# A sixth weight tile for the experts, placed in memory that the router has given back, and scaled outputs moved to a shared scratch tile

## The chip, the cores and the metric

The kernel runs on one core of a Trainium2 chip. The metric is device microseconds of one execution, the median of several; lower is better. In the text PE is the matmul engine (PEld its weight load), DVE the vector engine, ACT the scalar engine, POOL GpSimd, and SP the sync engine, whose queue issues nearly all weight loads.

## The reference

Two blocks run one after the other on 256 tokens of width 1024, all in float32. The first block (depth 1) is a mixer of three branches, a cross attention and a feed-forward layer. The second block has two layers, each a token mixer and then a mixture of experts, which is the part that matters here:

```
def hierarchical_moe(h, w_grp, b_grp, w_exp, b_exp, w_gate, w_up, w_down):
    ...
    for gi in range(N_GROUPS):
        sl = slice(gi * EXPERTS_PER_GROUP, (gi + 1) * EXPERTS_PER_GROUP)
        hid = jax.nn.silu(jnp.einsum('td,edf->tef', t, w_gate[sl])) * jnp.einsum('td,edf->tef', t, w_up[sl])
        y = y + jnp.einsum('tef,efd->td', hid * combine[:, sl, None], w_down[sl])
```

Each layer has 32 experts. An expert has three matrices of 1024 x 256 floats (1 MiB each). The router picks two experts for every token, and `combine` holds their weights. The result is scaled per column by a gate vector and added to x.

## The kernel before

All 96 expert matrices of a layer are read once, whatever the router picks. `ExpertLoads` reads them in loads of three matrices, one from each of three experts in a row: gate 0, up 0, then for j = 1 to 10 gate j, down j-1, up j, and last down 10. These are 33 loads for a layer; a load is three DMAs of 1 MiB (two for j = 10), all issued by SP. A load goes into a tile of three places, 24 KiB in each partition. Five such tiles (`ring0` to `ring4`) are used in turn, so a load has to wait until the matmuls have finished with the tile that it overwrites. In this text "load n" counts these loads from 1 in each layer.

SP runs its queue in order. Three loads are issued while the mixer before is still at work, two more (`for _ in range(2): loads.load()`) when the last memory of the mixer comes free. The router then works: logits, the best group, the two best experts, ranks of tokens within an expert, and the weights `comb`. Its tiles are in a pool `pro`, opened as `pr`. The last of these tiles to be read is `csel`, in the reduction at L1751, inside the first step of `group(0)`.

The work on the experts goes in 11 groups j of three experts and a fourth set of slots for overflow, 32 token slots each. `group(j)` gathers the tokens of the slots into `XT` with one-hot matrices `Sg`; `gate(j)` and `up(j)` multiply them with the weights (L1631), `mid(j)` transposes, `down(j)` multiplies with the third matrix (L1815), and `scatter(j)` adds the outputs to four banks `yb` over all groups. The order on PE is written out by hand: gate(j), group(j+1), down(j-1), up(j), scatter(j-1), mid(j). After each down product DVE scales half the output by the gate vector (`od`, L1821), ACT rounds it to a high part (`oh`, L1822), and DVE makes the low part (`ol`, L1823). The pool `pmoe`, opened after the router, holds these tiles twice.

`junk` is one scratch tile of 128 x 1024 for the whole kernel, and `jf` a pair of 128 x 256 scratch tiles. At the end of a layer a branch tests whether an expert got more tokens than its slots hold; if so, `overflow` works through all experts again. In the profiled execution it is not entered.

Of the kernel before, what the change touches and what calls it, by code (L numbers as in the profile page):

```python
# [9 lines left out]
F32 = mybir.dt.float32  # L10
# [5 lines left out]
P = 128  # L16
S = 256
D = 1024
# [120 lines left out]
class Net:  # L139
# [1520 lines left out]
    def moe(self, l):  # L1660
        tc, nc, V, C = self.tc, self.nc, self.V, self.C
        v, act, te = nc.vector, nc.scalar, nc.tensor
        A, x, ident, mod = self.A, self.x, self.ident, self.mod[l]
        with ExitStack() as c:
# [4 lines left out]
            ring = [(c, self.ctx)[l].enter_context(tc.tile_pool(name="ring%d" % i, bufs=1, side="right", reuse_waits="tile"))  # L1669
                    for i in range(5)]  # L1670
# [3 lines left out]
            loads = self.ExpertLoads(self, l, 3)  # L1674
# [13 lines left out]
            idx = pe.tile([P, 12], I32, name="idx")  # L1688
            for _ in range(2):
                loads.load()  # L1690
            pr = c.enter_context(tc.tile_pool(name="pro", bufs=1, reuse_waits="tile"))


            wg = pr.tile([P, KT, 40], F32, name="wg")
# [35 lines left out]
            route = self.route(l, pr, lg, comb, rank, sel, idx)  # L1730
            next(route)
            yb = [[self.bank("yb") for _ in range(2)] for _ in range(2)]
            pm = c.enter_context(tc.tile_pool(name="pmoe", bufs=2, reuse_waits="tile"))
            hold = {}

            def group(j):
# [39 lines left out]
            def weights(j):  # L1776

                w = loads.get()
                return [w[:, bass.ds(ats[j], 1)].rearrange("p o n -> p (o n)")] + [w[:, i] for i in (0, 1, min(2, 31 - 3 * j))]
# [28 lines left out]
            def down(j, hd):  # L1808
                wds = weights(j)
                bks = [self.bank(), self.bank()]  # L1810
                for h in range(2):
                    for f in range(2):
                        for i in range(4):
                            ps = slice(i * 32, i * 32 + 32)
                            te.matmul(bks[h][ps, :], hd[:, f, ps], wds[i][:, f * D + h * 512:f * D + h * 512 + 512],  # L1815
                                      start=f == 0, stop=f == 1)
                os = []
                for h in range(2):
                    t = pm.tile([P, 512], F32, name="od")
                    o = Split(pm.tile([P, 512], F32R, name="oh"), pm.tile([P, 512], F32R, name="ol"))  # L1820
                    v.tensor_tensor(t, bks[h], self.gb[:, h * 512:h * 512 + 512], op=OP.mult)  # L1821
                    act.activation(o.hi, t, AF.Copy)  # L1822
                    v.tensor_tensor(o.lo, t, o.hi, op=OP.subtract)  # L1823
                    os.append(o)
                return os
# [9 lines left out]
                skip_runtime_bounds_check_because="idx is 2 a + b of two flags of which at most one is set")  # L1835
            for _ in group(0):
                pass
            self.gb = self.gate_rows(pe, l, 1)
            with tc.manual_schedule(engines={mybir.EngineType.PE}):
                for j in range(12):  # L1840
                    if j < 11:
                        th = gate(j)
                    for _ in group(j + 1) if j < 10 else ():
                        pass
                    if j:
                        os = down(j - 1, hd)
                    if j < 11:
                        up(j, th)
                    if j:
                        scatter(j - 1, ST, os)  # L1850
                    if j < 11:
                        hd, ST = mid(j, th)
# [24 lines left out]
    def overflow(self, l, pm, xn, ga, bb, comb, rank, sel):  # L1877

        tc, nc, C, A = self.tc, self.nc, self.C, self.A
        v, act, te = nc.vector, nc.scalar, nc.tensor  # L1880
        x = self.x
        co = pm.tile([P, 2, 33], F32, name="co", bufs=1)
        cur = pm.tile([P, 1], F32, name="cur", bufs=1)
        c4 = co.rearrange("p t (j i) -> p t j i", i=3)
        v.scalar_tensor_tensor(c4, sel.unsqueeze(1).to_broadcast([P, 2, 11, 3]), -32.0, rank[:, :, :, 1:],
                               op0=OP.mult, op1=OP.add)
        v.scalar_tensor_tensor(co, co, 32.0, comb, op0=OP.is_ge, op1=OP.mult)
        v.tensor_scalar(co, co, 0.5, None, op0=OP.mult)
        v.memset(cur, 0.0)
        with tc.For_i(0, 32, 1) as e:  # L1890
            hT, wg, wu, wd, th = [self.wtile() for _ in range(5)]
            self.rest = []
            hT = hT.rearrange("p (k t) -> p k t", k=KT)
            for tt in range(2):
                for k in range(KT):
                    bk = self.bank()
                    te.transpose(bk[:, :P], xn[:, tt, k], self.ident)
                    v.tensor_scalar(hT[:, k, tt * P:(tt + 1) * P], bk[:, :P], ga[:, k:k + 1], bb[:, k:k + 1],
                                    op0=OP.mult, op1=OP.add)
            for w, nm, k, n in ((wg, "w_gate_2", 8, 256), (wu, "w_up_2", 8, 256), (wd, "w_down_2", 2, D)):  # L1900
                nc.sync.dma_start(w[:, :2048].rearrange("p (k n) -> p k n", k=k),
                                  A[nm][l, bass.ds(e, 1)].rearrange("o (p k) n -> p (o k) n", p=P))
            cv = pm.tile([P, 2], F32, name="cv", bufs=1)
            t = pm.tile([P, 2, 32], F32, name="ct2", bufs=1)
            for tt in range(2):
                v.scalar_tensor_tensor(t[:, tt], C["iota"][:, :32], cur, co[:, tt, :32], op0=OP.is_equal, op1=OP.mult)
            v.tensor_reduce(cv, t, axis=AX.X, op=OP.add)
            v.tensor_scalar(cur, cur, 1.0, None, op0=OP.add)
            th = th[:, :2 * S].rearrange("p (f t) -> p f t", f=2)
            bg, bu = self.bank(), self.bank()  # L1910
            for w, b in ((wg, bg), (wu, bu)):
                for f in range(2):
                    for k in range(KT):
                        te.matmul(b[:, f * S:(f + 1) * S],
                                  w[:, k * 256:(k + 1) * 256].rearrange("p (m f) -> p f m", f=2)[:, f], hT[:, k],
                                  start=k == 0, stop=k == KT - 1)
            tf = th.rearrange("p f t -> p (f t)")
            act.activation(tf, bg, AF.Tanh, scale=0.5)
            v.scalar_tensor_tensor(tf, tf, 1.0, bg, op0=OP.add, op1=OP.mult)
            v.tensor_tensor(tf, tf, bu, op=OP.mult)  # L1920
            for tt in range(2):
                for h in range(2):
                    sl = slice(h * 512, h * 512 + 512)
                    b = self.bank()
                    for f in range(2):
                        te.matmul(b, th[:, f, tt * P:(tt + 1) * P], wd[:, f * D + h * 512:f * D + h * 512 + 512],
                                  start=f == 0, stop=f == 1)
                    j = self.junk.tile([P, D], F32, name="junk")
                    v.scalar_tensor_tensor(j[:, :512], b, cv[:, tt:tt + 1], self.gb[:, sl], op0=OP.mult, op1=OP.mult)
                    v.tensor_tensor(x[:, tt, sl], x[:, tt, sl], j[:, :512], op=OP.add)  # L1930
# [31 lines left out]
```

## Time and profile before

| what | value |
|---|---|
| median of 3 runs | 1361.88 us (1358.8 to 1363.7) |
| the profiled execution's own time | 1359.46 us |
| its span, first to last instruction | 1357.6 us |
| PE busy | 1247.4 us (92%) |
| PEld busy | 995.8 us (73%) |
| DVE busy | 702.5 us (52%) |
| ACT busy | 554.7 us (41%) |
| bytes moved | 375.95 MB, mean 277 GB/s |
| mean granted TensorE clock | 0.963 |

Engine times overlap, so they do not add up to the span. A busy share is a mean over stages with different limits; the stage around the change is at about 690 to 930 us of the span for the first expert layer, and at about 1100 to 1350 us for the second.

### The profile page before, as it was taken

The page shows a single profiled execution, that of the slowest core. Times are in us where ns is not written, and L with a number is a line of the kernel's source. Part 1 is how long each engine was busy: PE and PEld are TensorE (multiplying, and loading weights), DVE is VectorE, ACT ScalarE, POOL GpSimd, SP SyncE. Part 2 cuts the span into 40 slices and gives each one's busy share as a digit, 9 for nine tenths or more (in the row PEclk, how much of TensorE's full clock was granted, in tenths as well). Part 3 has the DMA queues.
Part 4 walks back from the last instruction along what each step waited for, and adds up shares of the span by engine and source line. Part 5 has one row for each costly group of instructions (what it writes and reads, how often), then busy time and mean ns, then how long its engine had stood idle before and what let it go on. Part 6 is the DMA issues. An engine that isn't in the chain of part 4 may idle for free. (4 is left out here: it accounts for less than half of the span.)

```text
span 1357.6 us, 26598 instructions
## 1 busy us (share of the span) xinstructions
PE 1247.4 (92%) x11058; PEld 995.8 (73%) x11058; DVE 702.5 (52%) x1414; ACT 554.7 (41%) x1022; POOL 76.9 (6%) x91
## 2 busy tenths in 40 slices
PE   6999999999999999999989988777999989997985
PEld 6988899866999995788876655455888876665552
DVE  5797756545555554685553332325685554332223
ACT  5578546554444443446532221214445532221212
POOL 2000000000000001121100000001121100000000
PEclk9998999999999998999989999998999989998898
DMA  9553548769955555864368999999563466999994
GB/s 314 167 178 99 166 161 272 302 269 379 366 199 190 193 187 170 296 226 151 159 279 340 419 416 419 418 419 364 167 229 136 186 279 273 417 418 418 419 418 196
DMA packets 131947, 375.95 MB, mean 277 GB/s; under 512 B 7056, under 2 KB 90128, under 8 KB 100848
## 3 DMA queue, kind: packets, MB, share of 16 engines
q1 hardware_dynamic: 130080, 367.84, 72.0%
q0 software_dynamic: 1312, 5.21, 1.1%
q8 instruction: 91, 1.49, 0.4%
q10 hardware_dynamic: 432, 1.14, 0.2%
q14 instruction: 32, 0.26, 0.1%
HBM read 373.12 MB, written 1.05 MB: 276 GB/s over the span
## 5 line engine op out<-in xcount | busy, mean ns | idle before, releaser
L241 DVE TENSOR_TENSOR wlo<-w,whi 128x1024 fp32r<-128x1024 f32 x214 | 263.0, 1231 | 189.8 <-ACT whi L239 189.6
L239 ACT ACTIVATE whi<-w 128x1024 fp32r<-128x1024 f32 x214 | 225.7, 1056 | 269.1 <-PE bk L278 181.2
L277 PE MATMUL bk<-hTh,whi 128*128 128x256 f32 (+1 forms) x1128 | 321.7, 287 | 2.7 <-ACT whi L239 2.5
L278 PE MATMUL bk<-hTl,whi 128*128 128x256 f32 (+1 forms) x1128 | 317.1, 282 | 0.9 <-DVE hTl L384 0.7
L279 PE MATMUL bk<-hTh,wlo 128*128 128x256 f32 (+1 forms) x1128 | 316.3, 281 | 0.1
L277 PEld LDWEIGHTS bk<-hTh,whi 128*128 128x128 f32 (+1 forms) x1128 | 211.5, 188 | 21.0 <-issue 3.6
L278 PEld LDWEIGHTS bk<-hTl,whi 128*128 128x128 f32 (+1 forms) x1128 | 210.9, 187 | 3.3 <-DVE hTl L384 1.2
L279 PEld LDWEIGHTS bk<-hTh,wlo 128*128 128x128 f32 (+1 forms) x1128 | 210.8, 187 | 1.8 <-DVE kk L1421 0.8
L1631 PE MATMUL bk<-w,XT 128*32 128x256 f32 (+1 forms) x2816 | 173.7, 402 | 40.8 <-DMA w<-in_w_up 32.0
L1631 PEld LDWEIGHTS bk<-w,XT 128*32 128x32 f32 x2816 | 99.7, 116 | 115.5 <-issue 67.2
L1760 PEld LDWEIGHTS bk<-Sg,xn 128*128 128x128 f32 x704 | 83.1, 197 | 12.7 <-issue 12.7
L1760 PE MATMUL bk<-Sg,xn 128*128 128x128 f32 x704 | 87.2, 284 | 4.3 <-DVE Sg L1740 4.3
L1815 PE MATMUL bk<-w,hd 128*32 x704 | 81.7, 605 | 7.5 <-DMA w<-in_w_down 3.9
L1764 ACT ACTIVATE XT<-bk,modcol,gp 128x128 f32<-128x128 f32 x88 | 40.3, 458 | 77.8 <-DVE XT L1766 77.8
L1803 ACT ACTIVATE hd<-bk 128x256 f32<-128x256 f32 x22 | 8.4, 384 | 141.5 <-PE bk L1801 141.5
L1766 DVE TENSOR_SCALAR XT<-bk,gp,modcol 128x128 f32<-128x128 f32 x88 | 36.1, 410 | 45.9 <-PE bk L1760 33.3
L1815 PEld LDWEIGHTS bk<-w,hd 128*32 128x32 f32 x704 | 21.4, 111 | 49.7 <-issue 47.2
L1822 ACT ACTIVATE oh<-od 128x512 fp32r<-128x512 f32 x44 | 27.7, 629 | 68.6 <-DVE od L1821 68.6
L1787 DVE SCALAR_TENSOR_TENSOR mth<-mth,bk 128x256 f32<-128x256 f32 x22 | 9.3, 422 | 88.9 <-ACT mth L1786 88.9
L1055 PE MATMUL ada<-w,cact 128*32 128x512 f32 x384 | 51.8, 646 | 1.1 <-DMA w<-in_w_ada 1.1
L1793 DVE SCALAR_TENSOR_TENSOR mth<-mth,cslot,bk 128x256 f32<-128x256 f32 x22 | 10.6, 480 | 75.9 <-PE bk L1631 75.9
L1821 DVE TENSOR_TENSOR od<-bk,gb 128x512 f32<-128x512 f32 x44 | 30.3, 688 | 33.3 <-PE bk L1815 33.3
(511 smaller groups left out, 1958.2 us busy)
## 6 DMA issues: line engine op xcount, KB each, us to landing
w<-in_w_gate SPq DMA_DIRECT2D x64, 1024.0 KB, 19.8
w<-in_w_up SPq DMA_DIRECT2D x64, 1024.0 KB, 19.9
w<-in_w_down SPq DMA_DIRECT2D x64, 1024.0 KB, 19.9
w<-in_w_in SPq DMA_DIRECT2D x48, 1024.0 KB, 6.6
w<-in_w_ada SPq DMA_DIRECT2D x48, 1024.0 KB, 5.0
w<-in_w_ffn_in SPq DMA_DIRECT2D x22, 1024.0 KB, 11.4
w<-in_w_out SPq DMA_DIRECT2D x12, 1024.0 KB, 5.1
w<-in_w_ffn_out SPq DMA_DIRECT2D x11, 1024.0 KB, 6.8
```

Of the source, the lines that this page charges most:

```text
L239: self.nc.scalar.activation(W.hi, v, AF.Copy)
L241: self.nc.vector.tensor_tensor(W.lo, v, W.hi, op=OP.subtract)
L277: mm(out, l.hi, r.hi, start=start, stop=False)
L278: mm(out, l.hi, r.lo, start=False, stop=False)
L279: mm(out, l.lo, r.hi, start=False, stop=stop)
L1055: te.matmul(bk[q * 32:(q + 1) * 32, :], cact[:, k:k + 1].to_broadcast([P, 32]), w[:, q * 512:(q + 1) * 512], start=k == 0, stop=k == KT - 1)
L1631: self.nc.tensor.matmul(out[ps, :S], XT[:, k, ps], w[i][:, k * S:(k + 1) * S], start=k == 0, stop=k == KT - 1)
L1760: te.matmul(o, xn[:, tt, d], Sg[:, tt], start=tt == 0, stop=tt == 1)
L1764: act.activation(XT[:, d], o, AF.Identity, scale=gp[:, d:d + 1], bias=bp[:, d:d + 1])
L1766: v.tensor_scalar(XT[:, d], o, gp[:, d:d + 1], bp[:, d:d + 1], op0=OP.mult, op1=OP.add)
L1815: te.matmul(bks[h][ps, :], hd[:, f, ps], wds[i][:, f * D + h * 512:f * D + h * 512 + 512], start=f == 0, stop=f == 1)
L1821: v.tensor_tensor(t, bks[h], self.gb[:, h * 512:h * 512 + 512], op=OP.mult)
```

## The change

A sixth tile of the same size, `ring5`, is opened after the first gather, and load 6 is issued into it at that place of the program. To make room, the router's pool `pro` is opened after `pmoe` and closed before `ring5` is opened, so that `ring5` may lie where the router's tiles were. `od` is no longer two buffers of `pmoe` but the two halves of `junk`. The small tiles of `overflow` become columns of one `jf` tile, which is taken at the start of the layer.

```
@@ -1688,7 +1688,9 @@
             for _ in range(2):
                 loads.load()
-            pr = c.enter_context(tc.tile_pool(name="pro", bufs=1, reuse_waits="tile"))
+            self.small = self.junk.tile([P, S], F32, name="jf", bufs=2)
+            pm = c.enter_context(tc.tile_pool(name="pmoe", bufs=2, reuse_waits="tile"))
+            cr, (pr,) = self.scope(("pro", 1))
...
             yb = [[self.bank("yb") for _ in range(2)] for _ in range(2)]
-            pm = c.enter_context(tc.tile_pool(name="pmoe", bufs=2, reuse_waits="tile"))
             hold = {}
...
                 os = []
+                od = self.junk.tile([P, D], F32, name="junk")
                 for h in range(2):
-                    t = pm.tile([P, 512], F32, name="od")
+                    t = od[:, h * 512:h * 512 + 512]
...
             for _ in group(0):
                 pass
+
+            cr.close()
+            ring.insert(0, (c, self.ctx)[l].enter_context(tc.tile_pool(name="ring5", bufs=1, side="right", reuse_waits="tile")))
+            loads.load()
             self.gb = self.gate_rows(pe, l, 1)
...
-        co = pm.tile([P, 2, 33], F32, name="co", bufs=1)
-        cur = pm.tile([P, 1], F32, name="cur", bufs=1)
+        small = self.small
+        co = small[:, 0:66].rearrange("p (t e) -> p t e", t=2)
+        cur, cv = small[:, 66:67], small[:, 68:70]
+        t = small[:, 72:136].rearrange("p (t e) -> p t e", t=2)
```

SP's queue in the first expert layer, with the semaphores that each instruction waits for, from the second DMA of load 5 on; `idx` are the router's flags, `w_` with a number a weight tile, and names such as DMAHW0 count landings of DMAs. Before:

```order
L1651 DMA w_7402<-in_w_up_2 128x2048 [waits DMAHW6_49]
L1651 DMA w_7402<-in_w_up_2 128x2048 [waits DMAHW7_49]
L1861 TENSOR_LOAD idx_7397 [waits DVE_49]
L1861 ISA x2
L1651 DMA w_7901<-in_w_gate_2 128x2048 [waits DMAHW0_49,PE_49]
L1651 DMA w_7901<-in_w_gate_2 128x2048 [waits DMAHW1_49]
L1651 DMA w_7901<-in_w_gate_2 128x2048 [waits DMAHW2_49]
L1651 DMA w_7978<-in_w_down_2 128x2048 [waits DMAHW3_49,PE_49]
L1651 DMA w_7978<-in_w_down_2 128x2048 [waits DMAHW4_49]
```

And with the change:

```order
L1651 DMA w_7402<-in_w_up_2 128x2048 [waits DMAHW6_49]
L1651 DMA w_7402<-in_w_up_2 128x2048 [waits DMAHW7_49]
L1651 DMA w_7624<-in_w_gate_2 128x2048 [waits DMASW6_49,DVE_49,DMASW7_49,PE_49,DMAHW0_49,Activation_49,Pool_49]
L1651 DMA w_7624<-in_w_gate_2 128x2048 [waits DMAHW1_49]
L1651 DMA w_7624<-in_w_gate_2 128x2048 [waits DMAHW2_49]
L1651 DMA w_7982<-in_w_down_2 128x2048 [waits DMAHW3_49,PE_49]
L1651 DMA w_7982<-in_w_down_2 128x2048 [waits DMAHW4_49]
```

Load 6 (`w_gate` after load 5's `w_up`) now waits for other work of PE and for DVE, ACT and POOL too. SP's read of the flag for the branch has moved from ahead of load 6 to behind the last load, where it stands ahead of the next layer's `w_in` loads:

```order
L1651 DMA w_9358<-in_w_down_2 128x2048 [waits DMAHW7_49,PE_49]
L1651 DMA w_9358<-in_w_down_2 128x2048 [waits DMAHW0_49]
L1867 TENSOR_LOAD idx_7397 [waits DVE_49]
L1867 ISA x2
L224 DMA w_9696<-in_w_in_2 128x8x256 [waits DMAHW3_49,DMAHW2_49,DMAHW4_49,DMAHW1_49,PE_49]
```

The order on PE, DVE, ACT and POOL is the same as before. On DVE the scaled outputs of a down product read, before:

```order
L1821 TENSOR_TENSOR od_8668<-bk_8650,gb_7619 128x512 [waits PE_49]
L1823 TENSOR_TENSOR ol_8670<-od_8668,oh_8669 128x512 [waits Activation_49]
L1821 TENSOR_TENSOR od_8674<-bk_8651,gb_7619 128x512 [waits PE_49]
L1823 TENSOR_TENSOR ol_8676<-od_8674,oh_8675 128x512 [waits Activation_49]
L1793 SCALAR_TENSOR_TENSOR mth_8605<-mth_8605,cslot_8445,bk_8680 128x256 [waits PE_49]
```

and with the change:

```order
L1823 TENSOR_TENSOR junk_8668<-bk_8650,gb_7628 128x512 [waits PE_49]
L1825 TENSOR_TENSOR ol_8670<-junk_8668,oh_8669 128x512 [waits Activation_49]
L1823 TENSOR_TENSOR junk_8668<-bk_8651,gb_7628 128x512 [waits PE_49]
L1825 TENSOR_TENSOR ol_8675<-junk_8668,oh_8674 128x512 [waits Activation_49]
L1794 SCALAR_TENSOR_TENSOR mth_8605<-mth_8605,cslot_8446,bk_8679 128x256 [waits PE_49]
```

Nothing moved there; the two halves now share one buffer, and the waits are the same.

## Rows read from the trace of the kernel before

**Rows 1.** The page: DMA engines' busy tenths in 40 slices, and GB/s.

```profile
DMA  9553548769955555864368999999563466999994
GB/s 314 167 178 99 166 161 272 302 269 379 366 199 190 193 187 170 296 226 151 159 279 340 419 416 419 418 419 364 167 229 136 186 279 273 417 418 418 419 418 196
```

**Rows 2.** Windows around load 6, first layer: stretch, length, engines' busy time, clock, DMA share, GB/s.

```profile
709.00:710.00 1.00, 1.00 (x7) 1.00 (x7) 0.56 (x3) 0.00 (x0) 0.00 (x0) 0.55 1.00 418
710.00:711.00 1.00, 1.00 (x12) 1.00 (x11) 0.41 (x1) 0.17 (x1) 0.00 (x0) 1.00 0.42 172
...
717.00:718.00 1.00, 1.00 (x12) 0.94 (x9) 0.39 (x1) 0.38 (x1) 0.00 (x0) 1.00 0.00 0
718.00:719.00 1.00, 1.00 (x11) 1.00 (x11) 0.03 (x1) 0.00 (x0) 0.00 (x0) 1.00 0.72 139
719.00:720.00 1.00, 1.00 (x11) 1.00 (x11) 0.41 (x1) 0.41 (x1) 0.00 (x0) 1.00 0.92 369
```

**Rows 3.** The same windows around load 6 of the second layer.

```profile
1118.00:1120.00 2.00, 0.00 (x0) 0.03 (x1) 1.89 (x17) 0.00 (x0) 0.00 (x0) 0.50 0.48 197
1128.00:1130.00 2.00, 2.00 (x44) 1.04 (x32) 0.00 (x0) 0.06 (x1) 0.00 (x0) 1.00 0.04 8
1130.00:1132.00 2.00, 2.00 (x20) 1.88 (x17) 0.42 (x1) 0.38 (x1) 0.00 (x0) 1.00 0.46 82
1132.00:1134.00 2.00, 2.00 (x21) 2.00 (x19) 0.82 (x3) 0.86 (x2) 0.00 (x0) 1.00 0.91 381
```

**Rows 4.** Timeline of SP, first layer: start, length, instruction (loads 6, 7, two late).

```profile
717.19 1.28 SPq L1651 DMA_DIRECT2D w<-in_w_gate  x3
724.89 1.28 SPq L1651 DMA_DIRECT2D w<-in_w_down  x3
...
863.07 5.27 SPq L1651 DMA_DIRECT2D w<-in_w_gate  x3
870.56 5.26 SPq L1651 DMA_DIRECT2D w<-in_w_down  x3
```

**Rows 5.** Timeline of SP, second layer: loads 6 and 7.

```profile
1130.25 1.56 SPq L1651 DMA_DIRECT2D w<-in_w_gate  x3
1137.95 1.28 SPq L1651 DMA_DIRECT2D w<-in_w_down  x3
```

**Rows 6.** Timeline: the router's last work on ACT and DVE, both layers.

```profile
707.12 0.21 ACT L1611 ACTIVATE ge<-ge 128x8 f32<-128x8 f32 x1 [6.53 <-DVE w L1615]
...
709.38 0.23 DVE L1751 TENSOR_REDUCE comb<-csel 128x22 f32<-128x66 f32 x1
...
1122.49 0.22 DVE L1751 TENSOR_REDUCE comb<-csel 128x22 f32<-128x66 f32 x1
```

**Rows 7.** Timeline of PE, first layer: gate(0) and up(0).

```profile
713.47 3.66 PE L1631 MATMUL bk<-w,XT 128*32 x64
...
721.17 3.66 PE L1631 MATMUL bk<-w,XT 128*32 x64
```

**Rows 8.** Windows: the long stretch of each expert layer, columns as in group 2.

```profile
740.00:915.00 175.00, 151.12 (x1759) 97.28 (x1748) 51.01 (x130) 34.10 (x75) 0.00 (x0) 0.97 1.01 419
1150.00:1335.00 185.00, 164.12 (x1884) 103.39 (x1879) 55.04 (x137) 36.19 (x79) 0.00 (x0) 0.94 1.01 418
```

**Rows 9.** Timeline of PE near each layer's end, with the idle time before.

```profile
796.86 3.44 PE L1631 MATMUL bk<-w,XT 128*32 x60 [1.42 <-DMA w<-in_w_gate]
...
921.30 3.66 PE L1631 MATMUL bk<-w,XT 128*32 x64 [1.35 <-DMA w<-in_w_up]
...
1327.87 5.23 PE L1815 MATMUL bk<-w,hd 128*32 x32 [2.65 <-SPq L1862]
```

**Rows 10.** Timeline of DVE: scaled outputs of the last two groups, second layer.

```profile
1331.45 0.69 DVE L1821 TENSOR_TENSOR od<-bk,gb 128x512 f32<-128x512 f32 x1 [5.33 <-PE bk L1815]
...
1334.94 0.69 DVE L1823 TENSOR_TENSOR ol<-od,oh 128x512 fp32r<-128x512 f32 x1 [0.76 <-ACT oh L1822]
...
1341.52 0.69 DVE L1821 TENSOR_TENSOR od<-bk,gb 128x512 f32<-128x512 f32 x1 [4.42 <-PE bk L1815]
```

More of the change, by code (lines that the diff above doesn't have):

```diff
@@ L1902, in overflow @@
                                   A[nm][l, bass.ds(e, 1)].rearrange("o (p k) n -> p (o k) n", p=P))
-            cv = pm.tile([P, 2], F32, name="cv", bufs=1)
-            t = pm.tile([P, 2, 32], F32, name="ct2", bufs=1)
             for tt in range(2):
```

## The prediction

> **What bounds the kernel now.** The page's row of 40 slices comes first, since each slice is 33.9 us and the two expert layers stand out in it: the DMA engines are at nine tenths or more in slices 23 to 28 and 35 to 39, at 416 to 419 GB/s, and nowhere else for so long [rows 1]. The windows over the long stretch of each layer say the same more finely: DMA share 1.01 and 418 to 419 GB/s, while PE is busy 151.1 of 175 us and 164.1 of 185 us [rows 8]. So in these stretches the weights set the pace, and PE has 23.9 us and 20.9 us of idle time. PE first waits for a weight load in the first layer at 796.86 us, and still waits 1.35 us for `up` 10 at 921.30; in the second layer `down` 9 starts at 1327.87 after 2.65 us of waiting, which the view puts down to SP's branch, though what its matmuls need is a weight load, as in the first layer [rows 9]. The end of each layer is thus the end of the stream of loads plus a fixed tail.
>
> Then the question is whether that stream ever stops. The fine windows around load 6 show that it does. In the first layer the DMA share is 1.00 up to 710, 0.42 in the next microsecond, nothing at 717 to 718, then 0.72 and 0.92 [rows 2]. The five tiles are full; load 6 is issued at 717.19 [rows 4], which is 0.06 us after gate(0) has ended (713.47 + 3.66 = 717.13) [rows 7], because gate(0) reads the tile that load 6 overwrites. Counting 0.72 + 0.92 = 1.64 us of work up to 720, the stream restarts, in effect, at 718.36, 1.17 us after the issue. It stopped at 710.42. In the second layer it stops at 1118.96 (0.48 of two microseconds), load 6 is issued at 1130.25 [rows 5], and 0.92 + 1.82 = 2.74 us of work up to 1134 put the restart at 1131.26 [rows 3], 1.01 us after the issue. So about 7.9 us and 12.3 us of a transfer-bound stage pass without transfers.
>
> **The change part by part.** *Load 6 in the sixth tile.* It no longer waits for gate(0) but for what used the memory before: seven semaphores instead of two. The counts in the built program tell which instruction of each engine is meant. On DVE it is the reduction that reads `csel`; on ACT the router's first exponential, on PE the router's last rank product, on POOL the row norm, and the landings are of the mixer's constants and of an earlier expert load. The latest of these is the reduction: 709.38 + 0.23 = 709.61 in the first layer and 1122.49 + 0.22 = 1122.71 in the second; the exponential ended at 707.33 [rows 6]. How long SP takes from that to the issue is not in the trace for this pair; between 0.06 us (gate(0) to load 6) and, as an upper bound, the 1.17 us from issue to data, I take 0.15 us, near the first since it is the same queue and the same kind of wait. Load 6 is then issued at 709.76 and at 1122.86, and its data flow from 710.93 and 1123.87 on.
>
> A load of three places takes 870.56 - 863.07 = 7.49 us when the stream is full [rows 4]. Load 6 would be done at 718.42 and 1131.36. Load 7 now waits for gate(0), as load 6 did, so its data are ready to flow at 718.36 and 1131.26: no gap behind load 6. From then on every load is where the load before it was, so the stream is one load ahead, less what the issue comes late: 718.36 - 710.93 = 7.43 us and 1131.26 - 1123.87 = 7.39 us, under the ceiling of 7.49 us. Load 8 follows up(0) at about 724.9 as load 7 did [rows 4], early enough for a stream that ends load 7 at 725.9. **Sum: 14.8 us off.** With the upper bound for the wait (1.17 us) it would be 12.8 us; with no delay and a gain at the ceiling twice, 15.0 us.
>
> The Trainium skill bears on the length of a load. Its page "DMA: Bandwidth & Descriptors", section "Anatomy of one DMA — SWDGE (gpsimd) path", gives 2.0 us plus bytes over 436 GB/s for a DMA; the slope makes 7.2 us of 3.146 MB, and the sum would be 14.4 us. The trace has 7.49 us at 418 GB/s for a full load, and the sum above goes by that.
>
> *Is the gain passed on?* PE has 23.9 us and 20.9 us of idle time in the long stretches [rows 8]; 7.4 us earlier data leave 16.5 us and 13.5 us, so it meets its first missing load later than at 797 but still meets it, and the end still hangs on the stream. After the first layer the waits of the next `w_in` loads name the same matmuls as before, and these come 7.4 us earlier too.
>
> *Traffic beside the gather and gate(0).* It costs nothing: gate(0) ran without transfers and up(0) with the DMA share near 1.0 [rows 2], and each took 3.66 us [rows 7].
>
> *`od` in `junk`.* One buffer in place of two. The cover is the distance of groups: even in the last two, the closest, the chain of od, high part and low part runs from 1331.45 to 1335.63 and the next `od` begins at 1341.52 [rows 10], 5.9 us later. The halves of one group already alternate in DVE's order. Without the cover the chain of 4.18 us would stand in the path of a group; as it is, 0.
>
> *The router's pool behind `pmoe`, the columns in `jf`, SP's read of the flag.* The instructions of the router are the same and in the same order; the moved pool adds single waits for work of the mixer that is over. `jf` is only read in the branch that is not entered. The flag's read now stands ahead of `w_in`, which waits for the last groups anyway. I take 0 for all three; they could cost some tenths.
>
> From the profiled execution's own 1359.46 us (span 1357.6) that gives 1344.7 us, a span of 1342.8. The median of the runs is 2.4 us above that execution, which would make 1347.1. I say 1346.
>
> **The rivals.**
> *Only one layer gains.* If the wait for the `csel` reduction is longer in one of them, say by a landing not counted above, that layer's share is lost: 7.4 us, about 1353.5. Nothing in the rows speaks for it; the first layer is the tighter one, since the stream stops only 0.5 us before load 6 could flow.
> *No change.* If the new tile's memory is in fact held until gate(0) ends, load 6 stays at 717.19 and 1130.25, with load 7 right behind it. The stream then starts as before and is full as before: 1361. Against it speak the counts in the program.
> *Slower.* SP's queue is in order, and the new wait stands ahead of all 27 other loads of the layer. It hurts once it lasts beyond the end of gate(0). Were it to hold until up(0) ends (721.17 + 3.66 = 724.83 [rows 7]), the stream would restart 7.6 us late in each layer: 15 us more, about 1376. For it speaks that four engines are now waited for; against it that none of the instructions named comes later than 709.61.
> *PE becomes the bound.* If PE were to finish its groups later than the data arrive, part of the gain would be lost. That begins once its idle time in the long stretch is used up, which would need a lead of three loads, not one.
> *More than said.* If the clock of the last products changes: `down` 9 of the second layer took 5.23 us [rows 9], while up(0), with the same number of columns in all, took 3.66 us [rows 7]; the mean clock of that layer's long stretch is 0.94 against 0.97 [rows 8]. With the stream shifted against PE's work, such a run may be found at the full clock or another at the lower one: 1.6 us for each, which could add a little to the gain in both layers or take it away.
>
> **How the numbers follow.** Both layers gain, with the run-to-run spread of the shown runs (2 to 3 us either way) and the wait's upper bound: 0.80, between 1342 and 1350.5. One layer only: 0.08, 1351 to 1356. No change: 0.05. Slower: 0.04. More than 19 us: 0.03. The range from 1341.5 to 1352 holds the first case and the edge of the second. A difference of 0.3%, 4 us, is about what a measurement of this kernel can tell; the first two cases and the last are faster by more than that: 0.91. Same 0.05, slower 0.04.
>
> **What would show it.** Right: load 6 issued about 0.1 to 0.2 us after the `csel` reduction and 7.4 us ahead of gate(0)'s end; load 7 at gate(0)'s end; no window without transfers between load 5 and load 7 in the first layer and some 5 us instead of 12 in the second; the stretch from gate(0)'s start to the last down product shorter by 7.4 us in each layer; PE's first wait for a load later than 83.4 us (796.86 - 713.47) after gate(0)'s start. Wrong: load 6 issued at gate(0)'s end or later, a slower stream (a load over 7.5 us), or a layer whose last loads land earlier while its end does not move.

## Result and profile after

The changed kernel takes 1346.58 us (median of 4 runs, 1343.72 to 1351.89) against 1361.16 us: ratio 0.989, interval 0.9865 to 0.9917. Measured again beside its variants (6 runs): 1345.19 us, ratio 0.987, 0.9841 to 0.9903. Its profiled execution took 1347.01 us, with a span of 1345.2. Among the runs below, one of the kernel with the tile in the first layer alone took 1550.85 us at a granted clock of 0.742, where its others had 0.961 to 0.965; its ratio leaves that run out, its median does not.

The page's two DMA rows, 40 slices of 33.6 us, for the changed kernel:

```profile
DMA  9543448869965554965459999999563568999994
GB/s 314 168 163 117 144 158 269 326 235 386 367 220 189 188 189 141 316 221 188 188 205 399 419 417 419 419 419 378 179 229 132 216 258 331 418 418 418 419 418 186
```

Against [rows 1] the shape is the same: each expert layer is a plateau of 417 to 419 GB/s. The profiled execution moves 375.95 MB, as before, and in the plateaus as fast. The change is at the foot of the plateau, in the timeline of SP (start, length, instruction; loads 6 and 7 of the first layer, then of the second):

```profile
711.82 1.28 SPq L1651 DMA_DIRECT2D w<-in_w_gate  x3
719.31 1.31 SPq L1651 DMA_DIRECT2D w<-in_w_down  x3
...
1115.08 1.28 SPq L1651 DMA_DIRECT2D w<-in_w_gate  x3
1123.98 2.11 SPq L1651 DMA_DIRECT2D w<-in_w_down  x3
```

and in the timelines of DVE and PE, the `csel` reduction (now L1752), the first gather and gate(0) of both layers:

```profile
711.39 0.22 DVE L1752 TENSOR_REDUCE comb<-csel 128x22 f32<-128x66 f32 x1
...
708.90 5.36 PE L1761 MATMUL bk<-Sg,xn 128*128 128x128 f32 x32 [2.11 <-DVE Sg L1741]
...
715.59 3.66 PE L1631 MATMUL bk<-w,XT 128*32 x64
...
1114.66 0.22 DVE L1752 TENSOR_REDUCE comb<-csel 128x22 f32<-128x66 f32 x1
...
1112.17 6.75 PE L1761 MATMUL bk<-Sg,xn 128*128 128x128 f32 x32 [2.18 <-DVE Sg L1741]
...
1120.26 3.66 PE L1631 MATMUL bk<-w,XT 128*32 x64
```

Load 6 is issued 0.21 and 0.20 us after the reduction ends (711.61, 1114.88), and load 7 0.06 us after gate(0) ends (719.25, 1123.92), where load 6 stood before [rows 4, 5]. The windows around load 6 (columns as in [rows 2]), first layer and then second:

```profile
711.00:712.00 1.00, 1.00 (x6) 1.00 (x6) 0.56 (x3) 0.00 (x0) 0.00 (x0) 0.50 1.04 434
712.00:713.00 1.00, 1.00 (x11) 1.00 (x10) 0.41 (x1) 0.04 (x1) 0.00 (x0) 0.92 0.79 221
713.00:714.00 1.00, 1.00 (x12) 1.00 (x11) 0.41 (x1) 0.52 (x2) 0.00 (x0) 1.00 0.67 213
714.00:716.00 2.00, 2.00 (x19) 1.10 (x21) 1.37 (x6) 1.12 (x3) 0.00 (x0) 1.00 0.98 410
...
1111.00:1113.00 2.00, 0.83 (x4) 0.86 (x5) 2.00 (x17) 0.30 (x2) 0.00 (x0) 0.50 0.35 143
1115.00:1116.00 1.00, 1.00 (x7) 1.00 (x6) 0.04 (x1) 0.00 (x0) 0.00 (x0) 0.50 0.00 0
1116.00:1117.00 1.00, 1.00 (x7) 1.00 (x6) 0.47 (x2) 0.46 (x1) 0.00 (x0) 0.50 0.94 164
```

In the first layer the 7.9 us without transfers have become a dip (0.79 and 0.67 of the busy share, 221 and 213 GB/s: together half a microsecond by the share, one by the bytes); in the second some 4 us remain. The long stretches, and PE's first wait for a load in the first layer with the starts of up(10) in both:

```profile
740.00:907.00 167.00, 152.19 (x1780) 97.28 (x1776) 51.88 (x131) 34.37 (x75) 0.00 (x0) 0.96 1.01 418
1150.00:1320.00 170.00, 152.34 (x1762) 95.81 (x1760) 52.53 (x132) 34.84 (x77) 0.00 (x0) 0.96 1.01 418
```

```profile
814.80 3.66 PE L1631 MATMUL bk<-w,XT 128*32 x64 [0.39 <-DMA w<-in_w_gate]
...
916.11 3.66 PE L1631 MATMUL bk<-w,XT 128*32 x64 [1.35 <-DMA w<-in_w_up]
...
1320.14 3.66 PE L1631 MATMUL bk<-w,XT 128*32 x64 [1.39 <-DMA w<-in_w_up]
```

PE first waits 99.2 us after gate(0)'s start (814.80 - 715.59) instead of 83.4 us [rows 7, 9], but it still waits, and `up` 10 still waits for its load at the end: the layer is still as long as its stream.

The span is 12.4 us shorter. Cut at load 5's issue in each layer and at the first `w_in` issue between them, that is: 2.0 us later before the first layer (code that the change does not touch), 7.2 us off the first layer (225.24 to 218.04), 1.9 us off the mixer between (183.24 to 181.30, untouched too), and 5.2 us off the second layer with its tail (249.13 to 243.91). Over all profiles below the untouched mixer took 181.0 to 185.1 us and the first layer's load 5 came at 692.5 to 699.8, so 2 us of such a sum, and at times more, are chance. For sizes the next section uses a stretch with less of it.

### The profile page after: what moved, and what is told of

Its sections match the earlier page's. It is cut to its first block, busy times and chain, and to the rows that moved or that the text cites. A ratio compares the mean times of both kernels' runs of the same rounds, so it can differ in the third digit from the quotient of the medians.

```text
span 1345.2 us, 26608 instructions
## 1 busy us (share of the span) xinstructions
PE 1243.9 (92%) x11058; PEld 992.9 (74%) x11058; DVE 702.5 (52%) x1414; ACT 555.4 (41%) x1022; POOL 76.9 (6%) x91
## 2 busy tenths in 40 slices
DMA packets 131947, 375.95 MB, mean 279 GB/s; under 512 B 7056, under 2 KB 90128, under 8 KB 100848
## 5 line engine op out<-in xcount | busy, mean ns | idle before, releaser
L1824 ACT ACTIVATE oh<-junk 128x512 fp32r<-128x512 f32 x44 | 27.7, 630 | 65.2 <-DVE junk L1823 65.2
L1825 DVE TENSOR_TENSOR ol<-junk,oh 128x512 fp32r<-128x512 f32 x44 | 30.4, 691 | 31.6 <-ACT oh L1824 31.5
L1823 DVE TENSOR_TENSOR junk<-bk,gb 128x512 f32<-128x512 f32 x44 | 30.3, 688 | 30.2 <-PE bk L1816 30.2
```

## The experiments

Theory A is that of the prediction: behind load 6 the stream's place is set by load 7, which waits for gate(0)'s end, so all that counts is how much of load 6 has been moved by then. It is best read between two points of PE's timeline, the end of gate(0) and the start of up(10), which in most of them waits for the last load but one. Of all kernels, with the number of load 6's three DMAs issued before gate(0) ends (of the last two kernels, whose gate(0) and up(0) share a row, the end is load 7's issue less 0.06):

| kernel | DMAs early | first layer, us | second layer, us | median, us | ratio to before, 95% |
|---|---|---|---|---|---|
| before | 0 | 204.17 | 202.72 | 1360.5 to 1362.7 | |
| without the tile | 0 | 205.12 | 202.85 | 1361.38 | 0.9992 (0.9973 to 1.0011) |
| all three held | 0 | 203.94 | 202.56 | 1359.54 | 0.9986 (0.9968 to 1.0004) |
| two held, one early | 1 | 202.03 | 200.28 | 1356.04 | 0.9960 (0.9942 to 0.9978) |
| one held, two early | 2 | 199.24 | 197.85 | 1348.45 | 0.9895 (0.9870 to 0.9921) |
| first layer only | 3, 0 | 197.81 | 202.95 | 1355.10 | 0.9939 (0.9920 to 0.9958) |
| second layer only | 0, 3 | 203.94 | 196.28 | 1355.25 | 0.9959 (0.9938 to 0.9980) |
| changed kernel | 3 | 196.86 | 196.22 | 1346.58 | 0.9891 (0.9865 to 0.9917) |
| the same again | 3 | 198.11 | 196.33 | 1345.19 | 0.9872 (0.9841 to 0.9903) |
| gate(0) late | 3 | 196.67 | 196.06 | 1356.39 | 0.9963 (0.9941 to 0.9985) |
| load 6 earlier | 3 | 196.35 | 195.42 | 1345.83 | 0.9883 (0.9851 to 0.9915) |
| load 6 and gate(0) earlier | 3 | 198.45 | 196.49 | 1345.02 | 0.9875 (0.9843 to 0.9907) |
| up(0) first | 3 | 198.18 | 196.61 | 1347.32 | 0.9883 (0.9868 to 0.9898) |
| all three edits | 3 | 196.72 | 196.55 | 1344.24 | 0.9870 (0.9854 to 0.9886) |

**Without the tile.** The two lines that open `ring5` and issue load 6 are taken out; the rest of the change stays.

```diff
-            ring.insert(0, (c, self.ctx)[l].enter_context(tc.tile_pool(name="ring5", bufs=1, side="right", reuse_waits="tile")))
-            loads.load()
```

> Everything of the change but the sixth tile: od lies in junk, the router's pool is opened behind pmoe and closed early, the overflow's tiles are columns of jf; load 6 goes into the ring of five and waits for gate(0) again. Theory A (the whole gain is the stream of loads standing one load ahead): the time of before, 1361 us, from 1358 to 1363, load 6 issued at gate(0)'s end and 7 to 8 us and about 12 us without transfers in the two layers again. Theory B (part of the gain comes from od in junk, the order of the pools or the jf columns): clearly under before; half of the gain would be about 1354 us.

1361.38 us, no gain. `od` in `junk`, the pools' order and the `jf` columns are worth nothing that can be measured, and theory B falls.

**One layer only.** The same two lines under `if l == 0:` or `if l == 1:`.

> The sixth tile in the first expert layer alone; the second has a ring of five. Theory A: the first layer's share alone, 7.3 us by the stretch from gate(0)'s start to the next w_in issue in the two traces (206.5 to 199.2): 1361.2 - 7.3 = 1353.9 us, from 1352 to 1356. Theory C (one layer carries the gain): 1346.6 or 1361.

> The sixth tile in the second expert layer alone. Theory A: the second layer's share, 5.2 us by the stretch from load 5 to the output's DMA in the two traces (249.1 to 243.9), and 7.4 us if its first gather runs at the clock that it had in the kernel before: 1361.2 - 5.2 = 1356.0, or 1353.8 us; from 1352 to 1358. Theory C (one layer carries the gain): 1361 or 1346.6.

1355.10 and 1355.25 us: 6.7 and 6.6 us off by the medians, 8.3 and 5.6 us by the ratios (5.7 to 10.9 and 2.7 to 8.4 at 95%). Together that is 13.3 or 13.9 of the 14.6 to 15.4 us of the whole change. In the table the stretch is short only in the layer that has the tile. Both layers gain, so theory C falls.

**Two held, one early.** `ring5` is opened inside gate(0), and DVE copies one number of its product into the new tile before the load.

```diff
+                if after is not None:
+                    self.net.nc.vector.tensor_copy(t[0:1, 0, 0:1], after)
                 for i in range(min(3, 32 - 3 * j)):
...
+                if j == 0:
+                    ring.insert(0, (c, self.ctx)[l].enter_context(tc.tile_pool(name="ring5", bufs=1, side="right", reuse_waits="tile")))
+                    loads.load(b[0:1, 0:1])
```

> The sixth tile in both layers, but load 6 may not start before gate(0) has ended: DVE copies one number of gate(0)'s product into the tile first, and the load waits for that copy. The ring is six deep from there on and SP's read of the flag stands behind the last load, as in the changed kernel. Theory A: what counts is when the stream starts again, and that is gate(0)'s end as before: no gain, 1361 us plus some tenths for the copy, from 1359 to 1364. Theory D (the deeper ring or the moved read of the flag gives the gain, not the early start): as the changed kernel, 1346.6 us.

1356.04 us, which neither theory gave. The expectation was wrong about the kernel: the copy touches one of the tile's three places, and in SP's queue only the second DMA waits for it, with the third behind it. The first starts as early as in the changed kernel. SP's timeline of this kernel, load 6 as a group of three issues (start and length) and load 7, and a window before gate(0)'s end:

```profile
711.10 8.48 SPq L1653 DMA_DIRECT2D w<-in_w_gate  x3
719.67 1.55 SPq L1653 DMA_DIRECT2D w<-in_w_down  x3
```

```profile
717.00:718.00 1.00, 1.00 (x28) 0.60 (x20) 0.00 (x0) 0.00 (x0) 0.00 (x0) 1.00 0.04 16
```

The three issues stretch over 8.48 us, and at 717 the one early DMA is done and nothing moves. So this run became a third of a dose. A third of 7.49 us twice is 5.0 us; by the medians of this call it is 5.8 us (1361.84 to 1356.04), and by the table 2.3 and 2.5 us. It speaks for theory A by its size, and against theory D, since the ring is six deep here and SP's flag read stands behind the last loads, as in the changed kernel.

**All three held, and two early.** The copy goes into all three places, or into the third alone.

```diff
-                    self.net.nc.vector.tensor_copy(t[0:1, 0, 0:1], after)
+                    for i in range(3):
+                        self.net.nc.vector.tensor_copy(t[0:1, i, 0:1], after)
```

> As the kernel in which DVE copies one number of gate(0)'s product into the sixth tile, but now into each of its three places, so that none of load 6's three DMAs can start before gate(0) has ended. The ring is six deep. Theory A (the gain is what is transferred before gate(0) ends): nothing is, so the time of before, 1361 us, from 1359 to 1364. Theory D (the deeper ring gives part of the gain): clearly under 1359 us.

> The same, but the copy goes into the third place alone: two of load 6's three DMAs start early, as soon as the router's memory is free, and one waits for gate(0). Theory A: two thirds of the gain of 14.6 to 15.4 us, 9.7 to 10.3 us: 1351 us, from 1349.5 to 1353.5. Theory D: as the changed kernel or as with one DMA early, whatever the number of DMAs: 1346 or 1356 us.

Held wholly, it takes 1359.54 us, within 0.3% of before, and the second layer's stretch is 202.56 us against 202.72: a sixth tile that is not filled early is worth nothing. SP's flag read stands ahead of load 6 again in this kernel (at 706.5 and 1119.0 us; 706.5 and 1119.6 in the kernel before), so it is the deeper ring of theory D that falls here. The read has moved in the kernel with one DMA early, whose 2.5 us in the second layer are a third of 7.49 us and leave nothing for it. With two DMAs early it takes 1348.45 us, below the range expected (1349.5 to 1353.5): 13 us off where 9.7 to 10.3 were expected, from 4 runs. The table's stretches give 4.9 to 5.1 us for each layer, as expected. In the second layer one DMA after the other gives 2.5, 2.4 and 1.6 us (means 202.8, 200.3, 197.9, 196.2).

**The changed kernel again**, as a measure for the next three, which ran beside it.

> The changed kernel itself once more, as a measure for the three runs beside it, which differ from it by one edit each. 1346.6 us, from 1344 to 1349, by its first measurement.

1345.19 us, as expected.

**gate(0) late.** Six products ahead of gate(0) that nobody reads.

```diff
+                    if j == 0:
+                        late = self.bank()
+                        for n in range(6):
+                            te.matmul(late, C["ones"], xn[:, 0, 0:4].rearrange("p k t -> p (k t)"), start=n == 0, stop=n == 5)
                     if j < 11:
                         th = gate(j)
```

> The changed kernel with six more 128x512 products on PE right ahead of gate(0), whose result nobody reads; they make gate(0) end later and leave load 6 alone. Two such products of the gate rows took 1.13 us in the trace after, so about 3.4 us. Theory A (behind load 6 the stream's place is set by load 7, which waits for gate(0)'s end; there is no slack in either layer): load 7 is issued 3.4 us later in both layers and the end comes 6.8 us later, 1353.4 us, from 1351 to 1355. Theory F (once load 6 starts early, its own issue sets the stream, and load 7 has slack): no change, 1346.6 us.

PE's and SP's timelines of this kernel, first layer: the six products, gate(0), loads 6 and 7:

```profile
718.85 5.42 PE L1850 MATMUL bk<-xn,con 128*128 128x512 f32 x12
724.19 3.66 PE L1631 MATMUL bk<-w,XT 128*32 x64
```

```profile
714.83 1.28 SPq L1651 DMA_DIRECT2D w<-in_w_gate  x3
727.91 1.28 SPq L1651 DMA_DIRECT2D w<-in_w_down  x3
```

The products took 5.42 us, not 3.4; they contract over 128 rows, while the gate rows, from whose 1.13 us for two products they were reckoned, contract over one. By 5.42 us in two layers theory A gives 1345.2 + 10.8 = 1356.0 us; 1356.39 are measured. Load 6 still came at its early time, and load 7 13.08 us behind it. The stretch behind gate(0) is that of the changed kernel (196.67 and 196.06 us), though gate(0) is late: the whole rest of the layer hangs on gate(0)'s end. Theory F falls.

**Load 6 earlier.** The router's small tiles become columns of the spare `XT` buffer, so that load 6 waits for the logits only. (`Columns` hands out columns of that buffer; its code and two more such tiles are left out.)

```diff
+            few = Columns(pm.tile([P, KT, P], F32, name="XT").rearrange("p k t -> p (k t)"))
...
-            rstd = self.x_rstd(pr, "n5")
+            rstd = self.x_rstd(few, "n5")
...
-            route = self.route(l, pr, lg, comb, rank, sel, idx)
+            route = self.route(l, few, lg, comb, rank, sel, idx)
```

> The changed kernel with all small tiles of the router moved into the spare one of the two XT buffers, so that in the memory of ring5 only wg, xT and br lie. Load 6 then waits for the logits' scaling (ends at 1105.1 in the second layer of the trace after) instead of the csel reduction (1114.88), 9.8 us less, and follows load 5 with no gap. Theory A: load 7 still waits for gate(0)'s end, so the 4 us without transfers ahead of load 6 in the second layer come back behind it; at most 0.8 us in the first layer, where load 6 ends just as load 7's data begin: 1346 us, from 1344.5 to 1348. Theory F (load 6's issue sets the stream): 4.4 us off in the second layer and 0.5 us in the first, 1341.7 us.

SP's timeline and windows of this kernel, second layer:

```profile
1103.77 1.28 SPq L1651 DMA_DIRECT2D w<-in_w_gate  x3
1121.09 1.80 SPq L1651 DMA_DIRECT2D w<-in_w_down  x3
```

```profile
1112.00:1114.00 2.00, 2.00 (x12) 2.00 (x11) 1.31 (x8) 0.00 (x0) 0.00 (x0) 0.51 1.04 430
1118.00:1120.00 2.00, 2.00 (x45) 1.19 (x38) 0.00 (x0) 0.90 (x3) 0.00 (x0) 1.00 0.13 53
1120.00:1121.00 1.00, 1.00 (x21) 0.42 (x13) 0.00 (x0) 0.00 (x0) 0.00 (x0) 1.00 0.00 0
```

The gap ahead of load 6 is gone (430 GB/s at 1112) and has come back behind it (53 GB/s and none at 1118 to 1121). 1345.83 us beside 1345.19 for the changed kernel: no gain, as theory A has it.

**Load 6 and gate(0) earlier.** On top of that, the gate rows go behind gate(0), and seven products that nobody reads fill PE's idle time while the router works.

```diff
-            self.gb = self.gate_rows(pe, l, 1)
...
                         th = gate(j)
+                    if j == 0:
+                        self.gb = self.gate_rows(pe, l, 1)
...
+            def warm(n):
+                b = self.bank()
+                for i in range(n):
+                    te.matmul(b, C["ones"], x[:, 0, :512], start=i == 0, stop=i == n - 1)
...
+            warm(4)
             lg = few.tile([P, 2, 40], F32, name="lg")
...
             next(route)
+            warm(3)
```

> As the kernel with the early load 6, and gate(0) made earlier in two ways: the two products of the gate rows (1.13 us) go behind gate(0), and seven more 128x512 products on PE fill its idle time while the router works, to see whether the first gather then runs at the full clock (3.84 us as the second gather did, not 6.75 and 5.36 us at the lower one). Theory A: load 7 follows gate(0)'s end, so in the second layer the stream comes 1.1 us earlier without, and 1.1 + 2.9 = 4.0 us earlier with the full clock; in the first layer the stream has no gap left to close beyond 0.8 us. 1346.6 - 4.0 - 0.8 = 1341.8 us with the clock, 1344.7 us without. Theory F (load 6's issue sets the stream): the same as with the early load 6 alone.

1345.02 us, the same as the changed kernel within the interval of some 4 us either way; inconclusive as a time. PE's timeline of this kernel, second layer, and a window over its first gather (the third number from the end is the granted clock):

```profile
1112.52 3.81 PE L1785 MATMUL bk<-Sg,xn 128*128 128x128 f32 x32 [0.39 <-DVE Sg L1765]
```

```profile
1112.00:1117.00 5.00, 4.29 (x37) 4.09 (x36) 4.32 (x26) 1.24 (x5) 0.00 (x0) 1.00 1.01 418
```

The gather ran at the full clock. But from load 5 to gate(0)'s end it took 25.2 us in the second layer, against 26.8 in the changed kernel beside it and 27.8 in its first trace (19.8 against 22.5 in the first layer): 1.6 to 2.6 us, where 4.0 were expected against the first trace. Against the kernel beside it the gather (5.38 to 3.81 us) and the gate rows (1.13 us) should have made 2.7 us. In the second layer the gather began 16.9 us after load 5's issue instead of 16.4, and gate(0) then waited 0.48 us; whether the seven products hold the router up was not tried alone.

**up(0) first, and all three edits.** up(0) goes ahead of the second gather; the second kernel joins this with the early load 6 and puts the gate rows behind up(0).

```diff
                         th = gate(j)
+                    if j == 0:
+                        up(j, th)
                     for _ in group(j + 1) if j < 10 else ():
```

> The changed kernel with up(0) right behind gate(0) on PE, ahead of the second gather, so that load 8, which waits for up(0), is issued about 3.6 us after gate(0)'s end instead of 7.7. It is about the size of the gain: from gate(0)'s end to the start of up(10) it takes 202.8 us without an early DMA in the second layer, 200.3 with one, 197.9 with two and 196.2 with three, so the third DMA is worth 0.8 us less than the others. Theory G (with all of load 6 early, load 7 alone keeps the queue busy until about when load 8's data begin, and the stream loses some tenths there): the stretch falls by about 0.8 us to 195.4 us in the second layer, and likewise in the first; 1.6 us off the time, 1344 us. Theory H (the third DMA is worth less for another reason, such as a slower stream): the stretch stays at 196.2 us.

> What the runs point to, in one kernel: the router's small tiles in the spare XT buffer (load 6 early), the gate rows behind gate(0) (1.13 us), and up(0) right behind gate(0). Theory A: 1.1 us in the second layer from gate(0)'s earlier end, at most 0.8 us in the first, and 0.8 us in each layer if load 8's start was late: 1346 - 1.1 - 0.8 - 1.6 = 1342.5 us, from 1341 to 1345; without the last term 1344 us.

SP's timeline with up(0) first, loads 7 and 8 of the second layer, and PE's, up(10):

```profile
1125.59 1.28 SPq L1651 DMA_DIRECT2D w<-in_w_down  x3
1129.04 1.51 SPq L1651 DMA_DIRECT2D w<-in_w_up  x3
```

```profile
1322.14 3.66 PE L1631 MATMUL bk<-w,XT 128*32 x64 [1.39 <-DMA w<-in_w_up]
```

Load 8 is issued 3.5 us behind load 7, as meant, and up(10) still starts 196.6 us after gate(0)'s end. Theory G, which gave 195.4 us, falls: the third DMA is not worth less because load 8 came late. The two times, 1347.32 and 1344.24 us, cannot be told from the changed kernel's; no version beats it by what can be measured here.

## Why the prediction was right

**The bound** held. In the long stretches the loads still run at 418 GB/s, PE still waits for the last ones, and what was cut from the start of the stream came off the end.

**Load 6's wait** was read rightly from the semaphores: the `csel` reduction, with 0.20 to 0.21 us to the issue where 0.15 us were taken.

**Load 7 at gate(0)'s end** was right, and it is the step that carries the case: the kernel with gate(0) late lost 11.2 us, and the one with load 6 earlier won nothing.

**The sum, 14.8 us,** was the right mechanism with terms somewhat too large. By the table's means over kernels with none and with three DMAs early, the first layer gains 6.9 us (204.3 to 197.4) and the second 6.5 us (202.8 to 196.2): 13.4 us where 7.43 and 7.39 were forecast. The times say 14.6 and 15.4 us, with intervals of 11 to 18 and 13 to 22 us, so 13.4 is inside both, and the predicted 1346 us owes something to chance. The term that was mis-sized is "the stream is one load ahead, less what the issue comes late". The Trainium skill's page "DMA: Bandwidth & Descriptors", section "Anatomy of one DMA — SWDGE (gpsimd) path", gives a slope of 436 GB/s for DMAs that gpsimd issues; an estimate from it is 7.2 us for a load. The trace's full cadence, for loads that SP issues, is 7.49 us, and the measured lead lies under both.

Why 0.5 to 0.9 us for each layer are missing is open; the traces show when they are lost. Late in a layer SP issues a load of three DMAs every 7.48 us, as earlier ones land, so its issues show where the stream stands. Loads 16 and 33 of the second layer, of the kernel before and then of the changed one:

```profile
1191.63 5.27 SPq L1651 DMA_DIRECT2D w<-in_w_down  x3
...
1315.38 2.77 SPq L1651 DMA_DIRECT2D w<-in_w_down  x2
```

```profile
1178.88 5.27 SPq L1651 DMA_DIRECT2D w<-in_w_down  x3
...
1302.61 2.78 SPq L1651 DMA_DIRECT2D w<-in_w_down  x2
```

From gate(0)'s end (1130.19 and 1123.92) load 16 comes after 61.44 and 54.96 us, load 33 after 185.19 and 178.69, and up(10) after 202.72 and 196.22: the lead is 6.5 us all the way from load 16 to the end. In this pair what is missing was lost in the first 61 us. One place can be seen behind load 6, where the prediction had no gap:

```profile
1124.00:1125.00 1.00, 1.00 (x10) 1.00 (x11) 0.42 (x1) 0.37 (x1) 0.00 (x0) 1.00 0.61 115
1125.00:1126.00 1.00, 1.00 (x12) 1.00 (x11) 0.06 (x1) 0.00 (x0) 0.00 (x0) 1.00 0.52 139
```

Load 6 was issued 8.84 us ahead of gate(0)'s end, not 7.33 us as predicted, because the first gather took 6.75 us; so it was done before load 7's data flowed. That gap is not the whole cause. In the changed kernel measured again load 6 came 7.47 us ahead and no microsecond behind it fell so low (the lowest up to 1131 is 295 GB/s), yet the stretch is the same 196.33 us. Load 8's late start is not it either, by the kernel with up(0) first.

**Passed on** was right: PE's first wait came later, not never. **`od`, the pools, the `jf` columns** were rightly taken as 0, and the sixth tile without an early load too. SP's moved read of the flag was never tried alone, but it has moved in the kernels with one and with two DMAs held, whose stretches in the second layer leave nothing for it.

**Traffic beside gate(0)** costs nothing, as taken: with load 6 flowing gate(0) took 3.66 us in both layers, as without.

**The rivals**: one layer only and no change are excluded by the runs with one layer. The slower one, a wait that lasts past gate(0), did not come up. PE as the bound did not either: it kept 14.8 and 17.7 us of idle time in the long stretches.

**The clock**, in the prediction a rival for a larger gain, worked on another place. The changed kernel's second layer took 27.8 us from load 5 to gate(0)'s end, against 26.95 before; its first gather took 6.75 us, against 5.20. That is not the change's doing: measured again the gather took 5.38 us and the whole 26.8, and the kernel without the tile has 6.72 and 27.8.

## What to carry to other kernels

When a ring of tiles is filled by one queue in order, ask for each of the first loads what it waits for, and which of these waits comes last in time: that one sets the stream for the whole stage. An extra tile is worth what is transferred into it before that wait ends, up to one load, and nothing for being there; moving any other wait only moves the gap. Read such gains over a stretch between two fixed points of one engine, in several kernels, since untouched stages differ by 2 us and more from run to run.

## What the runs showed of the hardware

The busy share of the DMA engines is not bytes. In the first microsecond after a restart they show 0.94 at 164 GB/s (1116 to 1117 above), and 0.72 at 139 before [rows 2]. Counted in bytes at 418 GB/s, the stream restarts some 1.6 us after the issue (139 + 369 GB/s over 718 to 720 make 1.2 us of work: 718.8, issue 717.19), not 1.17 us as the prediction had it. The sum there took the difference of two restarts, so it hardly suffers.

While the router works PE has short products with pauses (in the changed kernel it was busy 0.90 of the 4 us from 1105 to 1109), and the granted clock falls to 0.50 (1.2 GHz). It stays there into the first gather, which takes 5.15 to 6.75 us in the profiles without extra products; the second, at 1.00 (2.4 GHz), takes 3.84. With seven products in the pauses PE was busy 3.59 of the 4 us from 1104 to 1108 in the second layer, the clock was 1.00 from there to the end of the first gather, and the gather took 3.81 us.
